# A streaming encoder layer on one core: order of the operand casts behind the last gate blocks, a tile ahead of the first branch products, the steps of operand loads, and a place for one copied sum

## The chip, the cores and the metric

The kernel runs on one core of one Trainium2 chip. The metric is the device time of one execution in microseconds; the time of a kernel is the median of its runs. Lower is better.

## The reference

One encoder layer for a prompt of 1024 tokens and a sample group of 32 tokens (1056 columns together), model width 1024, all in 32-bit floats. What matters here, cut down:

```python
h = rms_norm(x)
z = h @ w_in                        # q, k, v of branch A; q, f, i, og of branch B; gate_A, gate_B
ya = sliding_window_attention(...)  # branch A
yb = hgrn2_recurrence(...)          # branch B
mix = sigmoid(ga) * (ya @ w_br_a) + sigmoid(gb) * (yb @ w_br_b)
x = x + rms_norm(mix @ w_out)
a, u = split(rms_norm(x) @ w_up)    # each 2816 wide
x = x + rms_norm((gelu(conv3(a)) * u) @ w_down)
x = x + (p @ w_ple) * sigmoid(x @ w_ple_gate)
```

The change touches three borders: the end of the gate columns of `z`, the start of `ya @ w_br_a`, and the start of `rms_norm(x) @ w_up`.

## The kernel before, in words

**Products.** Every 32-bit operand is split in two parts, `hi` (a rounded cast, made by ACT) and `lo` (the rest, made by DVE), and a product of two such operands is three matmuls: hi by hi, hi by lo, lo by hi. Large products are taken as 2 x 2 blocks in a scheme of seven block products and some sums of operands and results, instead of eight. The columns (tokens) stand in four groups of H = 264. One product of a weight block with one group is 4 k-slices x 3 = 12 matmuls of 128 x 264.

**Gates.** `stream` (L252) multiplies a block of gate columns in two halves of 12 matmuls 128 x 384, into one PSUM bank; these appear in the trace as L205, L206, L207 with the banks called X, Y, Z. Behind a block, `gate_out` has ACT evict the bank with a tanh (L297, tile `gt`) and SP store it (L298, to `tb_d`). After each half m, `stream` runs the functions that `small[m]` lists. The last three blocks are `stream(tail[3:], small)`, so m counts 0 to 5, and what `small` lists is the preparation of branch A, put between the gates' own work:

- `a_prepare(n)` (L1514): makes weight blocks up to the n-th ready; a block is a cast on ACT (L1522, `wt<-wa`) and a subtraction on DVE (L1523). The raw blocks `wa` lie two to a tile in two tiles, which SP loads (L1512) when DVE has done with the blocks that lay there; `wt` has eight tiles. The order of the blocks is `A_ORDER` (L1496): for each column block c the products i = 0, 1, 2, later for each c the products 3 to 6.
- `a_split(i, p)` (L1540): operand i of column half p is split in place, a cast on ACT (L1537, `oa<-oa`) and a subtraction on DVE (L1538).
- `a_load(i, p)` (L1531): the load of an operand, L1534. The first five are issued by POOL before the stream, the rest by SP.

ACT, DVE and SP each run their instructions in the order in which they are listed for them; whoever waits holds what is listed behind it. `both` (L1543) lets the listed work of ACT and DVE be placed right behind what these engines were given last.

**Branch A.** `a_unit(ph, c, tps)` (L1593) takes two PSUM tiles X and Y of two banks each from the pool `pa` (tag `st`, three buffers). In phase 0 it makes product i = 0 in X, i = 1 in Y, and then adds i = 2 to X (L1620 hi·hi, L1622 hi·lo, L1624 lo·hi). Between the first and the third, ACT copies X to `as` (L1629), so that the product i = 2 cannot start before this copy; DVE makes `R` from Y and `as` (L1631), and after i = 2 it forms `ta` (L1634), a gate read back by SP (L1590, a ring of four tiles) times the product, which POOL stores to `mx_d` (L1635). The fifth load of `ta` needs the tile of the first, so it waits for the landing of the first store to `mx_d`. The units of phase 0 run in the order (c=0, p=0), (c=1, p=0), (c=0, p=1), (c=1, p=1), then c=2 and c=3 with both halves. In what follows X0 and Y0 are the tiles of the first unit, X1 and Y1 those of the second, and so on, and X1·i2 is the third product of the second unit. On PE the 12 matmuls of a product may be laid in pieces between those of others: before the change the order is X0·i0 12, Y0·i1 12, X1·i0 8, X0·i2 12, X1·i0 4, Y1·i1 12, X1·i2 12, so that 32 matmuls stand ahead of the first that needs `as`. After each product, `beside` runs the functions listed by `during(step, ...)` (L1676 ff): loads and splits of the operands 3 to 6.

**Up.** The up product has units of the same kind (L2304 hi·hi, L2305 hi·lo, L2306 lo·hi), with three PSUM tiles X, Y, Z. In `after` (L2311) ACT copies the first product from X to `s1c` (L2315), DVE makes `U2` (L2317), `nU3` (L2322) and from it a part of `us` (L2324). `s1c`, `U2`, `nU3` and `t12` are the four quarters of one page called `Sp` (L2178), which at this point holds an operand that DVE reads for the last time in L1902, the subtraction behind the cast of L1901. Just before, ACT copies a bank of the product with `w_ple` (L1948) and just behind it comes the output of the previous residual, `x` (ACT L1883, DVE L1888).

Of the kernel before, what the change touches and what calls it, by code (L numbers as in the profile page):

```python
# [10 lines left out]
F32 = mybir.dt.float32  # L11
# [3 lines left out]
ALU = mybir.AluOpType  # L15
AX = mybir.AxisListType

P = 128
# [12 lines left out]
H = 264  # L31
# [28 lines left out]
def layer_kernel(  # L60
# [21 lines left out]
    def right(name, bufs=1):  # L82
        return tc.tile_pool(name=name, bufs=bufs, side="right", reuse_waits="tile")

    dma, gdma = nc.sync.dma_start, nc.gpsimd.dma_start
    V, S, G, E = nc.vector, nc.scalar, nc.gpsimd, nc.tensor

    def behind(*engines):

        st = ExitStack()  # L90
        for e in engines:
            ins = next(i for i in reversed(nc.cur_bb.bb.instructions) if i.engine == e.engine)
            st.enter_context(tc.issue_after(ins))
        return st
# [185 lines left out]
    def unit(out):  # L280

        cell = []

        def get_w():
            if not cell:
                cell.append(next_w())
            return cell[0]
        return [(get_w, g, out) for g in range(3)]
# [4 lines left out]
    def gate_out(dst):  # L293
        def out(g, b):
            o, n = GR[g]
            t = gtile()
            S.activation(t[:, :n], b[:, :n], AF.Tanh, scale=0.5)  # L297
            dma(dst[:, o:o + n], t[:, :n])  # L298
        return out
# [17 lines left out]
    with right("ap") as ap:  # L317
# [279 lines left out]
        def pinned(f, *engines):  # L597
            with behind(*engines):
                f()
# [333 lines left out]
        blocks, small = [(lambda w=w: w, 2, out) for w, out in zip(ws, outs)], {}  # L933
# [125 lines left out]
    def b_prepare(n):  # L1059

        while n_b[0] < min(n + 1, 8 * NB):
            u, i = divmod(n_b[0], 8)
            if i == 0:
                if u not in raw_b:
                    b_raw(u)
                gens_b[u] = b_parts(u)
            next(gens_b[u])
            if i == 4 and u + 1 < NB:
                b_raw(u + 1)
            n_b[0] += 1  # L1070

    small = {2 * n: [lambda n=n: pinned(lambda: b_prepare(n), V)] for n in range(3)}
# [14 lines left out]
    with right("bp") as bp:  # L1087
# [309 lines left out]
        pieces, small = [], {}  # L1397
# [72 lines left out]
        u, v = (unit(gate_out(dst)) for dst, _ in GATES[14:])  # L1470
# [9 lines left out]
    def page(pool, n, shape, name):  # L1480

        s = f"{'r' if pool is rp else 'l'}{n}"
        s = home.get(s, s)
        return (rp if s[0] == "r" else lq).tile(shape, F32R, tag=f"pg{s[1:]}", name=nm(name))

    def page_at(s, shape, name):
        return page(rp if s[0] == "r" else lq, s[1:], shape, name)
# [40 lines left out]
    def a_page(i, p):  # L1528
        opa[i, p] = page_at(at_a[i][p], [P, 2, 4, H], "oa")

    def a_load(i, p, queue=dma):  # L1531
        t = opa[i, p]
        src = sa_d[i][:, :, p] if i in sa_d else ya_v[:, min(i, 1), i // 6][:, :, p]
        queue(t[:, 1].bitcast(F32), src)  # L1534
# [8 lines left out]
    def both(f, *a):  # L1543
        with behind(S, V):
            f(*a)

    small = {}
    first_a = [(i, p) for p in range(2) for i in range(3)]
    for i, p in [(3, 0), (3, 1), *first_a[::-1]]:
        a_page(i, p)  # L1550
    for i, p in first_a[:5]:
        a_load(i, p, gdma)
    for m, (i, p) in enumerate(first_a[:5]):
        small[m + 1] = [lambda i=i, p=p: both(a_split, i, p)]
    for n, m in enumerate((0, 0, 2, 3, 4, 5)):
        small.setdefault(m, []).append(lambda n=n: both(a_prepare, n))
    small[3].append(lambda: a_load(2, 1))
    stream(tail[3:], small)
    lctx.close()
# [4 lines left out]
    with right("mp") as mp:  # L1564
# [5 lines left out]
        pa = qctx.enter_context(  # L1570
            tc.tile_pool(name="pa", bufs=1, space=PSUM, reuse_waits="tile"))
# [2 lines left out]
            return bank(pt, "tr", 2)  # L1574

        Ra, Rb, Ya, Yb = [None] * 4, [None] * 4, [None] * 4, [None] * 4
        R_ = page_at("l6", [P, 4, 2, H], "R").bitcast(F32)

        tps_a = [(0, (0,)), (1, (0,)), (0, (1,)), (1, (1,)), (2, (0, 1)), (3, (0, 1))]
# [18 lines left out]
        def a_unit(ph, c, tps=(0, 1), ws=None, beside=None):  # L1598
# [9 lines left out]
            for n, i in enumerate(OPS[ph]):  # L1608
# [8 lines left out]
                for p in tps:  # L1617
                    o, x = t[:, p, 0:H], opa[i, p]
                    for k in range(4):
# [5 lines left out]
                                 skip_group_check=True)  # L1625
                x, r = t[:, sl, 0:H], R_[:, c, sl]
                if i == 0:
# [28 lines left out]
        def during(s, f, *a):  # L1656
            steps_a.setdefault(s, []).append((f, a))
# [12 lines left out]
            limit[0] = n_mix  # L1670
            both(load_next)

        for n, (i, p) in enumerate((i, p) for i in (4, 5, 6) for p in range(2)):
            a_page(i, p)
            during(2 * n, a_load, i, p)
            during(9 + n + n // 2, both, a_split, i, p)  # L1676
        for p in range(2):
            during(p, a_load, 3, p)
        for n, (i, p) in enumerate(((2, 1), (3, 0), (3, 1))):
            during(2 * n + 1, both, a_split, i, p)  # L1680
        for n in range(4):
            during(18 + n, y_load, n // 2, n % 2)
            during(23 + n, both, y_split, n // 2, n % 2)
# [104 lines left out]
    fo = foctx.enter_context(right("fo"))  # L1788
# [385 lines left out]
    octx.close()  # L2174
    fctx = ExitStack()
    fp = fctx.enter_context(right("fp"))
    us0 = fp.tile([P, T + 2], F32, tag="a", name="us0", bufs=2)[:, 0:T]
    Sp = page(lq, 3, [P, 4, 2, H], "Sp")  # L2178
    s1c, U2, nU3, t12 = (Sp[:, i].bitcast(F32) for i in range(4))
# [107 lines left out]
    def up_unit(u):  # L2287
# [4 lines left out]
        us4 = us.rearrange("p (a h c) -> p a h c", a=2, h=2)  # L2292
# [15 lines left out]
        def v(t, ps):  # L2308
            return t[:, ps[0]:ps[-1] + 1, 0:H]

        def after(i, ps):  # L2311
            x, y, zz = v(X, ps), v(Y, ps), v(Z, ps)
            sl = slice(ps[0], ps[-1] + 1)
            if i == 0:
                S.copy(s1c[:, sl], x)  # L2315
            elif i == 1:
                V.tensor_tensor(U2[:, sl], s1c[:, sl], y, op=ALU.subtract)  # L2317
            elif i == 2:
                V.tensor_tensor(ab[:, 2:2 + T].rearrange("p (a h c) -> p a h c", a=2, h=2)[:, sl, 0, :],
                                x, rb4[:, sl, 0, :], op=ALU.mult)  # L2320
            elif i == 3:
                V.tensor_tensor(nU3[:, sl], y, s1c[:, sl], op=ALU.subtract)  # L2322
            elif i == 4:
                V.tensor_tensor(us4[:, sl, 1, :], nU3[:, sl], zz, op=ALU.subtract)  # L2324
            elif i == 5:
                V.tensor_tensor(us4[:, sl, 0, :], y, s1c[:, sl], op=ALU.subtract)
            elif i == 7:

                S.copy(t12[:, sl], zz)
            elif i == 8:  # L2330
                V.tensor_tensor(nU3[:, sl], nU3[:, sl], t12[:, sl], op=ALU.add)
            else:
                V.tensor_tensor(t12[:, sl], U2[:, sl], zz, op=ALU.add)
# [465 lines left out]
    y = ys[1, 3]  # L2799
# [55 lines left out]
def build(shapes):  # L2855
    import concourse.bacc as _bacc

    nc = _bacc.Bacc("TRN2", target_bir_lowering=False, num_devices=1)
    args = [nc.dram_tensor(f"in_{n}_dram", s, F32, kind="ExternalInput").ap() for n, s in shapes]
    for i, shape in enumerate(_OUTS):  # L2860
        args.append(nc.dram_tensor(f"out_{i}_dram", shape, F32, kind="ExternalOutput").ap())
    with tile.TileContext(nc) as tc:
        layer_kernel(tc, *args)
    return nc
# [10 lines left out]
```

## Time and profile before

| | |
|---|---|
| median of 3 runs | 1948.23 us (1948.08, 1948.23, 1950.14) |
| the profiled execution's own time | 1950.0 us |
| its span | 1948.2 us (1.8 us lie outside the span) |
| PE busy | 1927.2 us, 99% |
| DVE, ACT, POOL busy | 75%, 52%, 16% |
| granted TensorE clock | 0.999 |

Times in the trace count from the start of the span. A row of the timeline has start, duration, engine, line, operation, output and inputs, and in brackets how long the engine was idle before it and what released it. A row of SP or POOL with `DMA_DIRECT2D` is the issue of a transfer, not the transfer.

### The profile page before, as it was taken

What the parts mean: (1) busy time and instruction counts of PE and PEld (TensorE: products, weight loads), DVE (VectorE), ACT (ScalarE), POOL (GpSimd) and SP (SyncE); (2) the same over time, 40 slices, a digit from 0 to 9 for tenths busy, and PEclk for the clock granted to TensorE, in tenths of its full rate; (3) what the DMA queues carried; (4) which work ended last, traced back from release to release, by engine and by line L of the source; (5) the groups of instructions that cost most, each with busy time, mean ns of one, the idle gap of its engine ahead of it and who ended that gap; (6) DMA issues with size and microseconds to landing.
All of it is one profiled execution on the core that took longest, in us unless ns stands there. A gap on an engine that the chain in (4) does not pass through costs nothing. (4 is left out here: it accounts for less than half of the span.)

```text
span 1948.2 us, 38057 instructions
## 1 busy us (share of the span) xinstructions
PE 1927.2 (99%) x14619; PEld 1910.0 (98%) x14619; DVE 1453.3 (75%) x3160; ACT 1012.4 (52%) x2182; POOL 307.3 (16%) x419
## 2 busy tenths in 40 slices
PE   8999999999999999999999999999999999999998
PEld 8999999999999999999999999999999999999998
DVE  6777777788888888657755778788787786768872
ACT  7667777666666666553324763333333336534432
POOL 2111111010101110100001123343543410000000
PEclk9999999999999999999999999999999999999999
DMA  8534543434637563487748582444565357654342
GB/s 269 156 108 122 139 121 97 139 104 103 155 113 166 96 120 75 124 292 226 219 148 289 182 290 92 140 131 152 131 147 148 104 179 235 220 185 153 115 132 87
DMA packets 310507, 302.19 MB, mean 155 GB/s; under 512 B 14293, under 2 KB 276344, under 8 KB 310325
## 3 DMA queue, kind: packets, MB, share of 16 engines
q1 hardware_dynamic: 277269, 229.57, 37.8%
q0 software_dynamic: 32928, 70.14, 15.8%
q8 instruction: 115, 1.88, 0.4%
q14 instruction: 67, 0.55, 0.1%
q10 hardware_dynamic: 128, 0.06, 0.0%
HBM read 213.48 MB, written 115.16 MB: 169 GB/s over the span
## 5 line engine op out<-in xcount | busy, mean ns | idle before, releaser
L2304 PE MATMUL st<-op,wt 128*128 128x264 f32 x1232 | 348.8, 283 | 2.1 <-ACT Sp L2315 1.4
L2306 PE MATMUL st<-op,wt 128*128 128x264 f32 x1232 | 349.7, 284 | 0.0
L2305 PE MATMUL st<-op,wt 128*128 128x264 f32 x1232 | 347.7, 282 | 0.0
L2304 PEld LDWEIGHTS st<-op,wt 128*128 128x128 f32 x1232 | 231.2, 188 | 3.5 <-ACT Sp L2315 2.0
L2305 PEld LDWEIGHTS st<-op,wt 128*128 128x128 f32 x1232 | 231.3, 188 | 0.0
L2306 PEld LDWEIGHTS st<-op,wt 128*128 128x128 f32 x1232 | 230.8, 187 | 0.0
L2428 PE MATMUL st<-dop,wt 128*128 128x264 f32 x616 | 174.4, 283 | 1.4 <-ACT S L2443 1.4
L2430 PE MATMUL st<-dop,wt 128*128 128x264 f32 x616 | 174.3, 283 | 0.0
L2429 PE MATMUL st<-dop,wt 128*128 128x264 f32 x616 | 173.9, 282 | 0.0
L1972 ACT CAST wt<-wu 128x512 fp32r<-128x512 f32 x126 | 76.0, 619 | 177.7 <-POOL wu L1981 70.9
L205 PE MATMUL mm<-La,wh 128*128 128x384 f32 (+1 forms) x480 | 158.2, 330 | 0.0
L206 PE MATMUL mm<-Lb,wh 128*128 128x384 f32 (+1 forms) x480 | 155.3, 324 | 0.6 <-DVE Lb L781 0.4
L207 PE MATMUL mm<-La,wl 128*128 128x384 f32 (+1 forms) x480 | 154.9, 323 | 0.1
L1973 DVE TENSOR_TENSOR wt<-wu,wt 128x512 fp32r<-128x512 f32 x126 | 86.4, 694 | 44.9 <-ACT wt L1972 44.9
L2428 PEld LDWEIGHTS st<-dop,wt 128*128 128x128 f32 x616 | 115.6, 188 | 1.9 <-ACT S L2443 1.6
L2429 PEld LDWEIGHTS st<-dop,wt 128*128 128x128 f32 x616 | 115.7, 188 | 0.0
L2430 PEld LDWEIGHTS st<-dop,wt 128*128 128x128 f32 x616 | 115.4, 188 | 0.0
L2078 ACT CAST wt<-wd 128x512 fp32r<-128x512 f32 (+1 forms) x84 | 49.1, 586 | 91.7 <-PE st L2430 71.9
L206 PEld LDWEIGHTS mm<-Lb,wh 128*128 128x128 f32 x480 | 90.4, 189 | 1.7 <-DVE Lb L781 1.4
L207 PEld LDWEIGHTS mm<-La,wl 128*128 128x128 f32 x480 | 90.2, 188 | 0.5 <-DVE wl L756 0.5
L1119 PE MATMUL G<-La,wt 128*128 128x288 f32 x288 | 90.4, 314 | 0.0
L205 PEld LDWEIGHTS mm<-La,wh 128*128 128x128 f32 x480 | 90.2, 188 | 0.2
(602 smaller groups left out, 6240.8 us busy)
## 6 DMA issues: line engine op xcount, KB each, us to landing
wu<-in_w_up_dram SPq DMA_DIRECT2D x42, 512.0 KB
wu<-in_w_in_dram SPq DMA_DIRECT2D x36, 512.0 KB
w_d<-in_w_down_dram POOLq DMA_DIRECT2D x24, 704.0 KB, 6.9
a_d<-Up SPq DMA_DIRECT2D x22, 528.0 KB
wr<-in_w_in_dram SPq DMA_DIRECT2D x21, 512.0 KB
s_d<-sm SPq DMA_DIRECT2D x40, 264.0 KB
dop<-s_d SPq DMA_DIRECT2D x16, 528.0 KB
wr<-in_w_out_dram SPq DMA_DIRECT2D x16, 512.0 KB
```

Source lines behind the costliest of these rows:

```text
L205: E.matmul(ps, wh, a, start=first and n == 0, stop=False)
L206: E.matmul(ps, wh, b, start=False, stop=False)
L207: E.matmul(ps, wl, a, start=False, stop=last and n == len(ks) - 1)
L1119: E.matmul(o, wh, x[0][k], start=first and k == 0, stop=False, skip_group_check=True)
L1972: S.copy(t[:, 0], src)
L1973: V.tensor_tensor(t[:, 1], src, t[:, 0].bitcast(F32), op=ALU.subtract)
L2304: E.matmul(o, wh, xh, start=first and k == 0, stop=False, skip_group_check=True)
L2305: E.matmul(o, wh, xl, start=False, stop=False, skip_group_check=True)
L2306: E.matmul(o, wl, xh, start=False, stop=k == 3, skip_group_check=True)
L2428: E.matmul(o, wh, xh_, start=first and k == 0, stop=False, skip_group_check=True)
L2429: E.matmul(o, wh, xl_, start=False, stop=False, skip_group_check=True)
L2430: E.matmul(o, wl, xh_, start=False, stop=k == ng - 1, skip_group_check=True)
```

## The change

Four edits. (1) `small` is filled by one table instead of two rules. (2) A tile `st_gate` is taken from the pool `pa` ahead of the first unit, and is not used. (3) The loads of the operands 3 to 6 and their splits get other steps; the loads of operand 3 move from steps 0 and 1 to 1 and 3, the others from 0, 2, 4, 6, 8, 10 to 4, 5, 6, 8, 9, 11. (4) For the first half of the first up unit, the copied sum `s1` lies in a tile of its own (`s10`, in a buffer of the pool `fo` that was used for squares) instead of a quarter of `Sp`.

```diff
-    for m, (i, p) in enumerate(first_a[:5]):
-        small[m + 1] = [lambda i=i, p=p: both(a_split, i, p)]
-    for n, m in enumerate((0, 0, 2, 3, 4, 5)):
-        small.setdefault(m, []).append(lambda n=n: both(a_prepare, n))
+    for m, at_m in enumerate(((0, 1, (0, 0), (1, 0)), ((2, 0), 2), ((0, 1),), ((1, 1), 3), (4,), (5,))):
+        small[m] = [lambda x=x: both(a_prepare, x) if isinstance(x, int) else both(a_split, *x)
+                    for x in at_m]
     small[3].append(lambda: a_load(2, 1))
...
+        pa.tile([P, 2, 512], F32, tag="st", name="st_gate", bufs=3)
...
-        for n, (i, p) in enumerate((i, p) for i in (4, 5, 6) for p in range(2)):
-            a_page(i, p)
-            during(2 * n, a_load, i, p)
-            during(9 + n + n // 2, both, a_split, i, p)
-        for p in range(2):
-            during(p, a_load, 3, p)
-        for n, (i, p) in enumerate(((2, 1), (3, 0), (3, 1))):
-            during(2 * n + 1, both, a_split, i, p)
+        for i in (4, 5, 6):
+            for p in range(2):
+                a_page(i, p)
+        for n, (i, p) in enumerate((i, p) for i in (3, 4, 5, 6) for p in range(2)):
+            during((1, 3, 4, 5, 6, 8, 9, 11)[n], a_load, i, p)
+            during((5, 7, 9, 10, 12, 13, 15, 16)[n], both, a_split, i, p)
+        during(1, both, a_split, 2, 1)
...
+    s10 = fo.tile([P, H], F32, tag="sqz0", name="s10")
...
+            s1 = s10[:, :].unsqueeze(1) if u == 0 and ps == (0,) else s1c[:, sl]
             if i == 0:
-                S.copy(s1c[:, sl], x)
+                S.copy(s1, x)
             elif i == 1:
-                V.tensor_tensor(U2[:, sl], s1c[:, sl], y, op=ALU.subtract)
+                V.tensor_tensor(U2[:, sl], s1, y, op=ALU.subtract)
```

The other two readers of `s1c` in `after` get `s1` in the same way.

What this makes of the programs: every engine has the same number of instructions before and after. PE, ACT, DVE and SP have other orders at the start of branch A, POOL the same order; from the middle of branch A on the programs differ in the place of `s1` alone. The first tile X0 lies in the same PSUM banks (2 and 3) in both programs, and its first matmul waits for the same semaphores of ACT.

On ACT, from the third weight block to the second `as`, the order before is this. `wt_10920`, `wt_10940`, `wt_10962`, `wt_10982`, `wt_11038` and `wt_11057` are blocks 3 to 8 in the order of `A_ORDER`; `oa_10852`, `oa_10851`, `oa_10850` and `oa_10849` are the operands (2, 0), (0, 1), (1, 1) and (2, 1); `gt` is the eviction of the last gate block, and the brackets name the semaphores that an instruction waits for (DMAHW and DMASW are transfers).

```order
L1522 CAST wt_10920<-wa_10876 128x512
L1537 CAST oa_10852<-oa_10852 128x1056 [waits DMASW6_49]
L1522 CAST wt_10940<-wa_10876 128x512 [waits DMAHW6_49]
L1537 CAST oa_10851<-oa_10851 128x1056 [waits DMASW7_49]
L1522 CAST wt_10962<-wa_10917 128x512 [waits DMAHW7_49]
L297 ACTIVATE gt_10977<-Z_10944 128x384 [waits DMAHW2_49,PE_49,Activation_49]
L1537 CAST oa_10850<-oa_10850 128x1056 [waits DMASW0_49]
L1522 CAST wt_10982<-wa_10917 128x512 [waits DMAHW0_49]
L1522 CAST wt_11038<-wa_10959 128x512 [waits DMAHW6_49]
L1537 CAST oa_10849<-oa_10849 128x1056 [waits DMAHW1_49]
L1629 COPY as_11031<-st_11017 128x264 [waits PE_49]
L1522 CAST wt_11057<-wa_10959 128x512 [waits DMAHW7_49]
```

And after, where `wt_10909`, `wt_10944`, `wt_10964`, `wt_10982`, `wt_11037` and `wt_11056` are blocks 3 to 8:

```order
L1522 CAST wt_10909<-wa_10876 128x512
L1537 CAST oa_10851<-oa_10851 128x1056 [waits DMASW7_49]
L297 ACTIVATE gt_10979<-Z_10948 128x384 [waits DMAHW2_49,PE_49,Activation_49]
L1537 CAST oa_10850<-oa_10850 128x1056 [waits DMASW0_49]
L1522 CAST wt_10944<-wa_10876 128x512 [waits DMAHW6_49]
L1522 CAST wt_10964<-wa_10906 128x512 [waits DMAHW7_49]
L1522 CAST wt_10982<-wa_10906 128x512 [waits DMAHW0_49]
L1629 COPY as_11032<-st_11018 128x264 [waits PE_49]
L1522 CAST wt_11037<-wa_10961 128x512 [waits DMAHW1_49]
L1537 CAST oa_10849<-oa_10849 128x1056
L1522 CAST wt_11056<-wa_10961 128x512 [waits DMAHW2_49]
L1629 COPY as_11095<-st_11075 128x264 [waits PE_49]
```

The eviction `gt` has moved ahead of two weight blocks, (2, 0) is done before this piece, and the first `as` stands ahead of block 7 (the first block of a raw tile that SP loads late) and of operand (2, 1).

On SP, from the raw tile of blocks 7 and 8 (`wa_10959`) to that of blocks 11 and 12 (`wa_11079`), the order before is this; `wa_11035` is the tile of blocks 9 and 10, `oa_11011` and `oa_11012` are operand 4.

```order
L1512 DMA wa_10959<-in_w_br_a_dram 128x4x128 [waits DVE_49]
L1512 DMA wa_10959<-wa_d_104 128x4x128 [waits DMAHW7_49]
L298 DMA tb_d_102<-gt_10977 128x384 [waits DMAHW0_49,Activation_49]
L1512 DMA wa_11035<-in_w_br_a_dram 128x4x128 [waits DMAHW1_49,DVE_49]
L1590 DMA ta_11005<-ta_d_87 128x264 [waits DMAHW2_49,PE_49]
L1590 DMA ta_11007<-ta_d_88 128x264 [waits DMAHW3_49]
L1590 DMA ta_11009<-ta_d_87 128x264 [waits DMAHW4_49]
L1534 DMA oa_11011<-sa_d_110 128x4x264 [waits DMAHW5_49]
L1512 DMA wa_11035<-in_w_br_a_dram 128x4x128 [waits DMAHW6_49]
L1590 DMA ta_11074<-ta_d_88 128x264 [waits DMAHW7_49]
L1534 DMA oa_11012<-sa_d_110 128x4x264 [waits DMAHW0_49,PE_49]
L1512 DMA wa_11079<-wa_d_104 128x4x128 [waits DMAHW1_49,DVE_49]
```

And after, with `wa_10961`, `wa_11034` and `wa_11077` as the tiles of blocks 7 and 8, 9 and 10, 11 and 12, and `oa_11012` as operand (4, 0):

```order
L298 DMA tb_d_102<-gt_10979 128x384 [waits Activation_49]
L1590 DMA ta_11006<-ta_d_87 128x264 [waits DMAHW7_49,PE_49]
L1590 DMA ta_11008<-ta_d_88 128x264 [waits DMAHW0_49]
L1512 DMA wa_10961<-in_w_br_a_dram 128x4x128 [waits DMAHW1_49,DVE_49]
L1512 DMA wa_10961<-wa_d_104 128x4x128 [waits DMAHW2_49]
L1590 DMA ta_11010<-ta_d_87 128x264 [waits DMAHW3_49]
L1512 DMA wa_11034<-in_w_br_a_dram 128x4x128 [waits DMAHW4_49,DVE_49]
L1512 DMA wa_11034<-in_w_br_a_dram 128x4x128 [waits DMAHW5_49]
L1590 DMA ta_11073<-ta_d_88 128x264 [waits DMAHW6_49]
L1534 DMA oa_11012<-sa_d_110 128x4x264 [waits DMAHW7_49]
L1590 DMA ta_11135<-ta_d_89 128x2x264 [waits DMAHW0_49,DMASW1_49,DVE_49]
L1512 DMA wa_11077<-wa_d_104 128x4x128 [waits DMAHW2_49,DMAHW1_49,DVE_49]
```

The load of blocks 7 and 8 has moved behind two `ta` loads, and the fifth `ta` load (`ta_11135`, which waits for a store of POOL, DMASW1) now stands ahead of the load of blocks 11 and 12; before, it stood behind it.

On PE the order after is X0·i0 12, Y0·i1 12, X1·i0 2, X0·i2 12, X1·i0 10, Y1·i1 12, X2·i0 8, X1·i2 12: 26 matmuls stand ahead of the first that needs `as`, and 68 ahead of the one that needs the second `as`.

At the start of the up product, ACT before has this order; `ple` is the last copy of the product with `w_ple`, `Sp_14698` the page with the quarter `s1c`, `x_14269` the residual's output.

```order
L1901 CAST op_14626<-z_13153 128x1056 [waits DVE_49]
L1901 CAST op_14629<-z_13153 128x1056
L1948 COPY ple_14663<-st_14678 128x528 [waits PE_49]
L2315 COPY Sp_14698<-st_14699 128x264 [waits DVE_49,PE_49]
L1883 ACTIVATE x_14269<-x_14269 128x1056 [waits DMASW4_49]
```

And after, with lines that stand one lower or higher in the file:

```order
L1900 CAST op_14627<-z_13154 128x1056 [waits DVE_49]
L1900 CAST op_14630<-z_13154 128x1056
L1947 COPY ple_14664<-st_14679 128x528 [waits PE_49]
L2316 COPY s_14698<-st_14701 128x264 [waits PE_49]
L1882 ACTIVATE x_14270<-x_14270 128x1056 [waits DMASW4_49]
```

Nothing has moved here; the copy no longer waits for DVE. On PE the first unit's products were X·i0 12, Y·i1 12, Z·i4 2, X·i2 12, Y·i3 12, Z·i4 10, Y·i5 12, Z·i6 12, and are now X·i0 12, Y·i1 12, X·i2 12, Y·i3 12, Z·i4 12, Y·i5 12, Z·i6 12.

More of the change, by code (lines that the diff above doesn't have):

```diff
@@ L2321, in after @@
             elif i == 3:
-                V.tensor_tensor(nU3[:, sl], y, s1c[:, sl], op=ALU.subtract)
+                V.tensor_tensor(nU3[:, sl], y, s1, op=ALU.subtract)
             elif i == 4:
@@ L2325, in after @@
             elif i == 5:
-                V.tensor_tensor(us4[:, sl, 0, :], y, s1c[:, sl], op=ALU.subtract)
+                V.tensor_tensor(us4[:, sl, 0, :], y, s1, op=ALU.subtract)
             elif i == 7:
```

## The prediction

> **What bounds the kernel now.** I read the page first, for the busiest engine:
>
> ```profile
> PE 1927.2 (99%) x14619; PEld 1910.0 (98%) x14619; DVE 1453.3 (75%) x3160; ACT 1012.4 (52%) x2182; POOL 307.3 (16%) x419
> ```
>
> PE works for 1927.2 of the 1948.2 us of the span. The change removes no matmul, so it can only win from the 21.0 us in which PE is idle. Next, PE's waits by line, at the lines that the change touches:
>
> ```profile
> PE st L1620 <- ACT as L1629: 1.6, 2, 1.4
> PE st L2304 <- ACT Sp L2315: 1.4, 2, 0.9
> ...
> PE st L1620 <- ACT gt L297: 1.3, 1, 1.3
> ...
> PE st L2304 <- DVE us L2324: 0.3, 1, 0.3
> ```
>
> That is 1.6 + 1.4 + 1.3 + 0.3 = 4.6 us, 0.24% of the time. Third, PE's timeline at the border from the gates to branch A:
>
> ```profile
> 843.95 0.33 PE L207 MATMUL Y<-La,wl 128*128 128x384 f32 x1
> ...
> 848.11 0.34 PE L207 MATMUL Z<-La,wl 128*128 128x384 f32 x1
> 849.77 0.39 PE L1620 MATMUL st<-oa,wt 128*128 128x264 f32 x1 [1.32 <-ACT gt L297]
> 850.00 0.28 PE L1622 MATMUL st<-oa,wt 128*128 128x264 f32 x1
> ...
> 853.64 0.28 PE L1622 MATMUL st<-oa,wt 128*128 128x264 f32 x1
> 855.27 0.39 PE L1620 MATMUL st<-oa,wt 128*128 128x264 f32 x1 [1.35 <-ACT as L1629]
> ...
> 875.13 0.39 PE L1620 MATMUL st<-oa,wt 128*128 128x264 f32 x1 [0.20 <-ACT as L1629]
> ```
>
> Three waits: for the eviction of the last gate block, for the first `as`, and a small one. From 850.00 to 853.64 there are 30 steps (matmuls 2 to 32 of the order), so a matmul costs 0.121 us; the first one after a wait is followed 0.23 later (849.77 to 850.00), so each wait costs 0.11 beyond itself.
>
> Why was ACT late? Its timeline there:
>
> ```profile
> 844.37 0.49 ACT L297 ACTIVATE gt<-Y 128x384 f32<-128x384 f32 x1 [2.79 <-PE Y L207]
> 844.75 1.07 ACT L1537 CAST oa<-oa 128x1056 fp32r<-128x1056 f32 x1
> 845.72 0.62 ACT L1522 CAST wt<-wa 128x512 fp32r<-128x512 f32 x1
> ...
> 848.71 0.61 ACT L1522 CAST wt<-wa 128x512 fp32r<-128x512 f32 x1
> 849.23 0.49 ACT L297 ACTIVATE gt<-Z 128x384 f32<-128x384 f32 x1
> ...
> 853.35 0.62 ACT L1522 CAST wt<-wa 128x512 fp32r<-128x512 f32 x1 [2.15 <-DMA wa<-in_w_br_a_dram]
> 853.88 1.07 ACT L1537 CAST oa<-oa 128x1056 fp32r<-128x1056 f32 x1
> 854.85 0.37 ACT L1629 COPY as<-st 128x264 f32<-128x264 f32 x1
> ```
>
> From 844.75 on ACT is busy without a gap, and the eviction of Z stands behind casts: it starts at 849.23, though PE's last matmul of Z ended at 848.45. The copy `as` stands behind the cast of block 7, which waits 2.15 us for its load, and behind another cast. In both places ACT does first what PE needs later.
>
> **Part 1: the eviction earlier.** On ACT an operand cast takes 0.97 to the next start (844.75 to 845.72), a block 0.52 (848.71 to 849.23), an eviction 0.38 (844.37 to 844.75). After, ACT does (1,0) at 844.75, (2,0) at 845.72, block 3 at 846.69, (0,1) at 847.21, and is free at 848.18. The earlier eviction started 0.09 after the end of its last matmul (843.95 + 0.33 to 844.37); so Z's starts at 848.54 and ends at 849.03. PE started 0.05 after it before, so 849.08 instead of 849.77: **0.69 saved**. The operands of these casts were loaded by POOL, which then stood idle for long (the row of 858.09 below), so (2,0) is there 0.5 us sooner. DVE's half of (2,0) and of block 3 is worked out below and is done by 848.9, before PE needs it.
>
> **Part 2: `as` ahead of block 7.** Behind the eviction ACT does (1,1) at 848.92, blocks 4, 5 and 6 at 849.89, 850.41 and 850.93, and `as` at 851.45, done at 851.82. PE, from 849.08, has 26 matmuls before it needs `as`: 849.08 + 0.11 + 26 x 0.121 = 852.34. So no wait is left. Before, PE's matmul 33 would have come at 853.76 and came at 855.27: 1.51 plus 0.11, **1.62 saved**.
>
> **Part 3: the up copy.** The rows of PE, ACT and DVE at that border:
>
> ```profile
> 1155.65 0.28 PE L2305 MATMUL st<-op,wt 128*128 128x264 f32 x1
> 1156.88 0.39 PE L2304 MATMUL st<-op,wt 128*128 128x264 f32 x1 [0.95 <-ACT Sp L2315]
> ...
> 1163.06 0.39 PE L2304 MATMUL st<-op,wt 128*128 128x264 f32 x1 [0.34 <-DVE us L2324]
> ```
>
> ```profile
> 1154.76 0.60 ACT L1948 COPY ple<-st 128x528 f32<-128x528 f32 x1
> 1156.44 0.38 ACT L2315 COPY Sp<-st 128x264 f32<-128x264 f32 x1 [1.07 <-DVE op L1902]
> ```
>
> ```profile
> 1153.93 2.42 DVE L1902 TENSOR_TENSOR op<-z,op 128x1056 fp32r<-128x1056 f32 x2 [1.06 <-ACT op L1901]
> ...
> 1158.81 1.26 DVE L1888 TENSOR_TENSOR x<-x 128x1056 f32<-128x1056 f32 x1 [1.53 <-ACT x L1883]
> 1160.10 0.43 DVE L2322 TENSOR_TENSOR Sp<-st,Sp 128x264 f32<-128x264 f32 x1
> ...
> 1162.58 0.42 DVE L2324 TENSOR_TENSOR us<-Sp,st 128x264 f32<-128x264 f32 x1
> ```
>
> The copy waited 1.07 for DVE to finish reading the page that it writes. With its own tile it goes when ACT is free: the `ple` copy ends at 1155.36, and on ACT the next start lies 0.1 ahead of such an end (the cast of 844.75 ends at 845.82, the next starts at 845.72). So it starts at 1155.25, 1.19 earlier. X·i2 then starts at 1155.69. The end is set by `us`, though: Z·i6 waits for it, and it stands on DVE behind L1888, which waits for ACT's `x`, next behind the copy, and whose own wait is for a store issued long before (1141.13):
>
> ```profile
> 1141.13 1.50 POOL L1851 DMA_DIRECT2D x_d<-x  x2 [2.15 <-DVE x L1850]
> ```
>
> That chain moves by the same 1.19, so Z·i6 starts at 1161.87 instead of 1163.06: **1.19 saved**. PE gets there at 1155.69 + 0.11 + 48 x 0.121 = 1161.61, so a wait of 0.26 stays: the 0.34 does not go.
>
> Gains: 0.69 + 1.62 + 1.19 = 3.50 us.
>
> **What these moves cost.** Three new things; their rows, DVE, then SP, ACT and POOL:
>
> ```profile
> 845.86 1.26 DVE L1538 TENSOR_TENSOR oa<-oa 128x1056 fp32r<-128x1056 f32 x1 [2.99 <-ACT oa L1537]
> 847.03 0.68 DVE L1523 TENSOR_TENSOR wt<-wa,wt 128x512 fp32r<-128x512 f32 x1
> ...
> 848.80 0.68 DVE L1523 TENSOR_TENSOR wt<-wa,wt 128x512 fp32r<-128x512 f32 x1
> ...
> 857.37 0.42 DVE L1634 SCALAR_TENSOR_TENSOR ta<-ta,st 128x264 f32<-128x264 f32 x1
> ```
>
> ```profile
> 849.51 0.39 SPq L1512 DMA_DIRECT2D wa<-in_w_br_a_dram  x1
> ...
> 863.92 0.52 SPq L1590 DMA_DIRECT2D ta<-ta_d  x1
> ...
> 881.23 0.38 SPq L1512 DMA_DIRECT2D wa<-in_w_br_a_dram  x1
> ```
>
> ```profile
> 884.53 0.62 ACT L1522 CAST wt<-wa 128x512 fp32r<-128x512 f32 x1 [0.17 <-DMA wa<-in_w_br_a_dram]
> ```
>
> ```profile
> 858.09 0.56 POOL L1635 DMA_DIRECT2D mx_d<-ta  x1 [30.92 <-DVE ta L1634]
> ```
>
> ```profile
> SPq L1590 <- DMA mx_d<-ta: 7.8, 3, 3.9
> ```
>
> (n1) *Blocks 7 and 8 come later.* SP may load them when DVE has done with block 4. Before, that was 848.80 + 0.68 = 849.48, and SP issued at 849.51. After, DVE does (1,0) at 845.86, then (2,0), block 3, (0,1), (1,1), block 4 at 1.17 an operand (845.86 to 847.03) and 0.60 a block (847.03 to 848.80 less one operand): block 4 at 851.14, done at 851.82. The load takes 3.30 (881.23 to 884.53) to 3.84 (849.51 to 853.35) from issue to cast, so block 7 is cast at 855.15 to 855.7, and then (2,1), block 8 and the second `as` follow, 0.52 + 0.97 + 0.52 + 0.37 = 2.38 later: 857.55 to 858.1. PE needs it after 68 matmuls, at 849.19 + 68 x 0.121 = 857.42. A wait of 0.1 to 0.7, with restart up to 0.8; none if the load is a little quicker. I take 0.4, between, nearer to the 3.30.
> [...]
>
> (n2) *The fifth `ta` load ahead of blocks 11 and 12.* It waits for the first store to `mx_d`, and before it was issued 5.83 after that store's issue (858.09 to 863.92). The store comes 0.72 after `ta` begins (857.37 to 858.09), and that 2.10 after the third product's start (855.27 to 857.37). After: 852.34 + 2.10 + 0.72 = 855.16, so the fifth load goes at 860.99 at the latest; the other end is that the store lands as soon as the quickest of these loads, 3.30, at 858.46. The blocks' load goes behind its 0.52, and block 11 is cast 3.30 to 3.84 later: 862.3 to 865.4. An operand cast and the fourth `as` follow, 0.52 + 0.97 + 0.37 = 1.86: 864.2 to 867.2. PE needs this `as` after 132 matmuls, 849.19 + 132 x 0.121 + 0.4 = 865.56. So 0 to 1.7; I take 0.3, as most of the stretch lies before the need.
>
> (n3) *The small wait at 875.13* stands behind a cast of operand 5, whose load stands behind another `ta` load as before. It may go with its restart (0.2 + 0.11 gained) or grow; the nearest row for growth is the 2.15 that ACT waited for a load at 853.35, of which 1.35 reached PE, 1.15 more than now. The stores and loads ahead of it move with PE, so I take 0.
>
> The loads of operand 3 at later steps cost nothing: on SP they keep their place, and their splits come later. The tile `st_gate` costs nothing: it issues no instruction, and X0 keeps its banks.
>
> Sum: 3.50 - 0.4 - 0.3 = **2.8 us**. The profiled execution would go from 1950.0 to 1947.2; the median of the runs shown lies 1.8 below it, so the median goes from 1948.23 to **1945.4**.
>
> **Rivals.** *New waits eat the gain.* n1 at 0.8 and n2 at 1.7 leave 1.0 (1947.2); with n3 at its 1.15 as well, it is a loss of 0.15 (1948.4). For it: each move of ACT's order makes DVE free a raw tile later. Against: all of it hangs on loads that take the longer of the two times. Chance 0.20.
> *All waits go.* The loads come in time (0 for n1 and n2), and 875.13 (0.31) and 1163.06 (0.34 + 0.11 less what of it part 3 holds) go too: 3.50 + 0.31 + 0.39 = 4.2, 1944.0. For it: with PE earlier by 2 us the stores come earlier too. Against: the two new loads stand later on SP than before. Chance 0.15.
> *Slower: SP held by a store.* SP issues in order, and `ta` loads that wait for stores to `mx_d` (7.8 us in 3 waits, 3.9 the longest) now stand ahead of the loads of blocks 11 and 12 and of operands 5 and 6. If two such waits of 3.9 reach PE whole, 2 x 3.9 - 3.50 = +4.3, 1952.5. It decides once a store's landing is later than the blocks that PE still has: PE has 132 matmuls, 16 us, before the first. In before PE met none of the 7.8. Chance 0.04.
> [...]
> *The other banks do part X0 from the gates*, against the built order: PE would go on at 848.28 instead of 849.08, 0.8 more, 1943.9. Chance 0.02, since the first matmul waits on ACT as before.
>
> **How the numbers follow.** Forecast 0.59, new waits 0.20, all waits gone 0.15, slower 0.04, banks 0.02. The range 1944.0 to 1948.4 runs from "all gone" to the far end of "new waits"; forecast and new waits alone hold 0.79, so the lower end has to reach to the third. About 0.2% (3.9 us) is what a measurement of this kernel can tell from no change: runs of before lie 2.06 us apart. The forecast and the new waits stay within it (0.79); all gone and banks pass it (4.2 and 4.3): faster 0.17; slower 0.04.
>
> **What would show it.** In the profile after: no wait of L1620 for the first `as`; L297's wait shorter by 0.7; the first matmul of branch A 0.6 to 1.0 behind the last of Z; the up unit's wait for L2316 at most 0.2, and the one for `us` still there. A wait for the second and fourth `as` of a few tenths shows n1 and n2; none shows the third case. The forecast is wrong if PE waits over 1 us anywhere between 850 and 885, if PE's first wait is gone wholly (banks), or if ACT's `x` at the up border waits for its load, which would hold `us`.

## The result and the profile after

| | changed | before |
|---|---|---|
| median of 22 runs | 1953.23 us | 1950.01 us |
| lowest, highest | 1949.76, 1955.63 | 1948.06, 1954.85 |
| ratio, 95% interval | 1.0014 (1.0008 to 1.0021) | |
| profiled execution, span | 1950.3, 1948.6 us | 1950.0, 1948.2 us |

The change makes the kernel 0.14% slower, about 2.7 us (1.6 to 4.1), where a gain of 2.8 was forecast; the two medians themselves lie 3.2 apart. With 22 runs instead of 3, the median of before is 1950.01 and no longer 1948.23.

PE's waits in the profile after, at the same lines, and one at the very start of the program, which was 0.4 in before:

```profile
PE st L1620 <- ACT as L1629: 2.3, 2, 1.4
...
PE mm L654 <- DMA x<-in_x_prompt_dram: 1.2, 1, 1.2
...
PE st L1620 <- ACT gt L297: 0.6, 1, 0.6
...
PE st L2304 <- ACT s L2316: 0.4, 1, 0.4
...
PE st L2304 <- DVE Sp L2318: 0.2, 1, 0.2
```

The gate wait has fallen from 1.3 to 0.6, the copy's at the up border from 0.95 to 0.4; but the waits for `as` are 2.3 instead of 1.6, and they lie elsewhere. PE's timeline:

```profile
848.63 0.34 PE L207 MATMUL Z<-La,wl 128*128 128x384 f32 x1
849.60 0.39 PE L1620 MATMUL st<-oa,wt 128*128 128x264 f32 x1 [0.63 <-ACT gt L297]
...
857.85 0.28 PE L1622 MATMUL st<-oa,wt 128*128 128x264 f32 x1
858.17 0.39 PE L1620 MATMUL st<-oa,wt 128*128 128x264 f32 x1
...
867.11 0.39 PE L1620 MATMUL st<-oa,wt 128*128 128x264 f32 x1 [0.91 <-ACT as L1629]
...
876.09 0.39 PE L1620 MATMUL st<-oa,wt 128*128 128x264 f32 x1 [1.44 <-ACT as L1629]
```

The first `as` is no longer waited for. The second costs a little (0.32 from 857.85 to 858.17 instead of 0.12), the fourth 0.91, and the fifth, the first of column block 2, has grown from 0.20 to 1.44. What ACT did ahead of each:

```profile
849.06 0.49 ACT L297 ACTIVATE gt<-Z 128x384 f32<-128x384 f32 x1 [0.24 <-PE Z L207]
...
851.97 0.38 ACT L1629 COPY as<-st 128x264 f32<-128x264 f32 x1
855.73 0.62 ACT L1522 CAST wt<-wa 128x512 fp32r<-128x512 f32 x1 [3.38 <-DMA wa<-in_w_br_a_dram]
...
865.18 0.62 ACT L1522 CAST wt<-wa 128x512 fp32r<-128x512 f32 x1 [2.37 <-DMA wa<-wa_d]
...
874.46 1.07 ACT L1537 CAST oa<-oa 128x1056 fp32r<-128x1056 f32 x1 [1.85 <-DMA oa<-sa_d]
875.44 0.59 ACT L1629 COPY as<-st 128x528 f32<-128x528 f32 x1
```

The eviction now starts 0.09 behind PE's last matmul of Z (848.63 + 0.34) and no longer stands behind casts; `as` goes ahead of block 7, at 851.97. But the copy at 875.44, for which PE waits, stands behind the cast of operand (5,1), and that one waits 1.85 for its load, though PE doesn't need (5,1) until much later. SP in after, where the fifth `ta` load goes at 860.49, the sixth at 865.81 and the load of (5,1) at 867.37:

```profile
860.49 0.52 SPq L1590 DMA_DIRECT2D ta<-ta_d  x1
861.12 0.55 SPq L1512 DMA_DIRECT2D wa<-wa_d  x1
...
865.81 1.51 SPq L1590 DMA_DIRECT2D ta<-ta_d  x1
867.37 0.72 SPq L1534 DMA_DIRECT2D oa<-sa_d  x1
```

And its waits from 830 to 880:

```profile
SPq L1590 <- DMA mx_d<-ta: 8.5, 3, 4.2
```

In before, SP issued the load of (5,1) at 866.28, ahead of the sixth `ta` load:

```profile
866.28 0.63 SPq L1534 DMA_DIRECT2D oa<-sa_d  x1
867.01 0.65 SPq L1590 DMA_DIRECT2D ta<-ta_d  x1
```

There ACT's cast of it waited 1.14 and started at 873.51:

```profile
873.51 1.08 ACT L1537 CAST oa<-oa 128x1056 fp32r<-128x1056 f32 x1 [1.14 <-DMA oa<-sa_d]
```

PE's last matmul of Z ended at 848.45 in before and at 848.97 in after. Counted from there, the load of (5,1) is issued 0.57 later after the change and its cast starts 0.43 later, while PE gets to the matmul that needs `as` 0.80 earlier (876.09 - 1.44 against 875.13 - 0.20). The last two make up the 1.24 by which the wait has grown. At the up border, PE and ACT after:

```profile
1156.68 0.39 PE L2304 MATMUL st<-op,wt 128*128 128x264 f32 x1 [0.40 <-ACT s L2316]
...
1173.33 0.39 PE L2304 MATMUL st<-op,wt 128*128 128x264 f32 x1 [0.19 <-DVE Sp L2318]
```

```profile
1155.74 0.60 ACT L1947 COPY ple<-st 128x528 f32<-128x528 f32 x1
1156.23 0.39 ACT L2316 COPY s<-st 128x264 f32<-128x264 f32 x1
```

The copy goes 0.49 behind `ple`, as worked out, and the wait for `us` is gone as well; 17 us behind the copy's wait there is a new one for `U2` (L2318).

### The profile page after: what moved, and what is told of

It is laid out like the page before. It is cut to its first block, busy times and chain, and to the rows that moved or that the text cites. A ratio compares the mean times of both kernels' runs of the same rounds, so it can differ in the third digit from the quotient of the medians.

```text
span 1948.6 us, 38055 instructions
## 1 busy us (share of the span) xinstructions
PE 1927.8 (99%) x14619; PEld 1910.3 (98%) x14619; DVE 1453.7 (75%) x3160; ACT 1011.8 (52%) x2182; POOL 307.1 (16%) x419
```

## The experiments

Theory A: the place of the waiting `ta` loads on SP, ahead of loads on which ACT's casts and so an `as` hang, takes back what the casts gain. Rivals: B, the later casts free the raw weight tiles late; C, the loss lies at the up border; D, it came with the chip of the first timing; E, the loads are slow in themselves, since the DMA engines are full; F (beside A), a long wait lowers the granted clock. Parts 1 to 4 are here the four edits of the change. Each ratio is to runs of before on the same chip, with its 95% interval; "own" is the time of the profiled execution.

**e1_casts** (part 1 alone)

```diff
+    for m, at_m in enumerate(((0, 1, (0, 0), (1, 0)), ((2, 0), 2), ((0, 1),), ((1, 1), 3), (4,), (5,))):
```

> Only the order of the casts is changed (part 1), the loads keep their old steps and the copied sum its old place. Theory A (the loss comes from the place of the waiting ta loads on SP, which the load steps set): here the fifth ta load stands behind the weight blocks 11 to 14, so PE has no wait for the fourth as, the gate wait is about 0.6 and the first as wait is gone: 1.5 to 2.3 us below before. Rival B (the later casts free the raw weight tiles later, so blocks come late): 1 to 3 us above before, with waits for the second and fourth as near 859 and 867 as in after.

0.9999 (0.9991 to 1.0008), own 1949.96. The gate wait is 0.63 and the first `as` is not waited for, so both gains are there; new waits of 0.71 at 862.00 and 0.54 at 874.56 take back 1.25, less the 0.20 of before. No loss as B has it, and less gain than A.

**e2_loads** (part 3 alone)

```diff
+            during((1, 3, 4, 5, 6, 8, 9, 11)[n], a_load, i, p)
+            during((5, 7, 9, 10, 12, 13, 15, 16)[n], both, a_split, i, p)
```

> Only the load steps are changed (part 3). Theory A: the fifth ta load stands ahead of operand (4,1) and the sixth ahead of blocks 13 and 14, PE keeps its waits of 1.3 and 1.35 and gets new ones of 1 to 2 us between 860 and 880: 2 to 4 us above before. Rival B: no change within 0.5 us.

1.0003 (0.9994 to 1.0012), own 1952.46. The first `as` wait is 0.61 instead of 1.35, the one at 875.93 is 0.99 instead of 0.20. The load steps alone lengthen the later wait by 0.79, as A says, but the first wait falls by 0.74, and the time is level with before, where A expected 2 to 4 us above and B no change. This profile is longer than that of before for two other reasons: PE is 1.3 us later by 60 us, where the programs are the same, and in a stage that the change doesn't touch it goes at half clock (0.50 from 1619.22 to 1622.63), behind this wait (in before 1.42 there, and a clock of 1.00 from 1619 to 1624):

```profile
1618.57 0.39 PE L2427 MATMUL st<-dop,wt 128*128 128x264 f32 x1 [1.84 <-ACT S L2442]
```

**e3_sums** (part 4 alone)

```diff
-                S.copy(s1c[:, sl], x)
+                S.copy(s1, x)
```

> Only the copied sum has a tile of its own (part 4). Theories A and B: the wait of 0.95 for the copy falls to 0.2 or 0.4, something later gives a part back, 0.4 to 1.2 us below before. Rival C (the loss of a usual execution lies at the up border, not in branch A): 1 to 3 us above before.

0.9997 (0.9988 to 1.0006), own 1952.73. The wait for the copy is gone and 0.42 comes at `U2`. C finds no support. This profile is 2.7 us longer than that of before for another reason: by 60 us, where both programs are the same, PE is already 3.6 us later (rows of PE in the two traces set side by side); one of the waits there is for x_prompt, 1.1 against 0.4.

**e4_casts_sums** (parts 1 and 4)

```diff
+    for m, at_m in enumerate(((0, 1, (0, 0), (1, 0)), ((2, 0), 2), ((0, 1),), ((1, 1), 3), (4,), (5,))):
...
+    s10 = fo.tile([P, H], F32, tag="sqz0", name="s10")
```

> Parts 1 and 4 together, the old load steps. Theory A: the two gains add, 2 to 3.3 us below before, and this is the best of the four. Rival B: 0 to 2 us above before. Rival C: above casts alone by 1 to 3 us.

0.9997 (0.9988 to 1.0006), own 1948.08, with one wait of 0.59 at 861.34 left in branch A. Below before in the median (1949.45 to 1950.34), but not beyond its interval.

**e5_after_again** (the changed kernel, no edit)

> The changed kernel once more, timed on this chip beside before. Theory A (the waiting ta loads on SP, with both the casts and the load steps changed): its profile again has 2 to 3.5 us of waits for the fourth as and the first as of column block 2 between 858 and 878, and it is 1 to 4 us above before. Rival D (the loss came with the chip of the first timing, whose granted clock was 0.998 in 7 of 22 runs): within 1 us of before here, with clocks of 0.999 and 1.0.

1.0011 (1.0002 to 1.0020): it is slower on another chip too, so D falls. Waits of 0.90 and 1.74.

**e6_ta_on_pool** (after, with the `ta` loads issued by POOL)

```diff
-                dma(t[:, z_], ta_d[c_].rearrange("p (t h c) -> p h t c", t=2, h=2)[:, h_, z_])
+                gdma(t[:, z_], ta_d[c_].rearrange("p (t h c) -> p h t c", t=2, h=2)[:, h_, z_])
```

> After, but the ta loads of branch A are issued by POOL, so that SP holds no wait for a store to mx_d. Theory A: blocks 11 to 14 and operand 5 are issued 2 to 5 us sooner, the waits of 0.91 and 1.44 go or fall below 0.3, 1.5 to 3 us below after. Rival D or a loss that lies in the landing times of the loads themselves: the waits stay, within 0.5 us of after.

1.0002 (0.9993 to 1.0011), own 1950.57. PE's waits in branch A:

```profile
850.88 0.39 PE L1620 MATMUL st<-oa,wt 128*128 128x264 f32 x1 [1.40 <-ACT gt L297]
...
868.30 0.39 PE L1620 MATMUL st<-oa,wt 128*128 128x264 f32 x1 [1.15 <-ACT as L1629]
```

The wait near 876 is gone, as A has it; the one for block 11 stays (1.15, at 868.30), and the gate wait is back (1.40), since there the eviction waits for an earlier store of `gt`. So A holds for the larger wait, and not for the one at 867. The time came down to that of before (e5, on the same chip, has 1.0011).

**e7_casts_loads** (parts 1 and 3)

```diff
+    for m, at_m in enumerate(((0, 1, (0, 0), (1, 0)), ((2, 0), 2), ((0, 1),), ((1, 1), 3), (4,), (5,))):
...
+            during((1, 3, 4, 5, 6, 8, 9, 11)[n], a_load, i, p)
```

> Parts 1 and 3 without the copied sum's own tile. Theory A: branch A as in after (waits of 2 to 3.5 us between 858 and 878), 0.3 to 0.6 us above after, 2 to 4 above before. Rival C (the up border costs something in a usual execution): 1 to 3 us below after.

1.0014 (1.0005 to 1.0023), own 1953.4. The loss is there without part 4 and without the tile of part 2, and not with either of parts 1 and 3 alone: the casts bring PE forward, the load steps put operand 5 back. The wait at 877.00 is 2.34, and the mean granted clock of the profiled execution is 0.998 (0.999 in before).

**e8_after_look, e13_after_look, e14_after_look** (the changed kernel, three more profiles, no edit)

> The changed kernel, a further profile. Theory A: the sum of PE's waits in branch A varies from profile to profile by 1 us or more, since each hangs on when a store lands. Rival D: it repeats within 0.3 us, and what varies is the start of the program, where PE waits for x_prompt.

> The changed kernel, another profile. If theory A with theory F explains the loss: a wait of 1.4 to 2.4 us near 876, and where it is over 2 us, a pitch of 0.22 behind it; the time is 1950 to 1951 without and 1952 to 1956 with the lower clock.

> As for the run before it: the time and the clock behind the wait go together; a profile above 1952 us without a lower clock near 876 speaks against theory F as the missing part.

Own 1952.13, 1951.40 and 1951.43. PE in e8, from the wait to the end of the slow stretch:

```profile
875.29 0.39 PE L1620 MATMUL st<-oa,wt 128*128 128x264 f32 x1 [2.33 <-ACT as L1629]
...
876.50 0.35 PE L1620 MATMUL st<-oa,wt 128*128 128x264 f32 x1
876.65 0.42 PE L1622 MATMUL st<-oa,wt 128*128 128x264 f32 x1
876.87 0.42 PE L1624 MATMUL st<-oa,wt 128*128 128x264 f32 x1
...
879.95 0.30 PE L1622 MATMUL st<-oa,wt 128*128 128x264 f32 x1
```

The same stretch in the windows of e8 and of after; the third number from the end is the granted clock:

```profile
875.00:880.00 5.00, 4.71 (x26) 4.71 (x27) 3.67 (x5) 2.38 (x5) 0.00 (x0) 0.66 1.08 312
```

```profile
875.00:880.00 5.00, 3.91 (x32) 3.92 (x33) 2.96 (x3) 2.53 (x4) 0.00 (x0) 1.00 1.11 327
```

From 876.65 to 879.95 there are 15 steps of 0.22 us instead of 0.121: 1.5 us lost while PE counts as busy, which no table of waits shows. In e13 and e14 the waits are as long, but the clock is 1.00 from 875.42 to 878.83 in e13, and the mean of e14's whole span is 1.000:

```profile
876.52 0.39 PE L1620 MATMUL st<-oa,wt 128*128 128x264 f32 x1 [2.64 <-ACT as L1629]
```

```profile
877.03 0.39 PE L1620 MATMUL st<-oa,wt 128*128 128x264 f32 x1 [2.08 <-ACT as L1629]
```

So the wait varies from 1.44 to 2.64 in five profiles of one kernel (1.74 in e5), and F holds for some of the long waits, not for all; the last section sets the rows side by side.

**e9_op5_early** (after, the load of (5,1) two steps sooner; on SP it only changes places with the sixth `ta` load)

```diff
-            during((1, 3, 4, 5, 6, 8, 9, 11)[n], a_load, i, p)
+            during((1, 3, 4, 5, 6, 6, 9, 11)[n], a_load, i, p)
```

> After, with the load of operand (5,1) two steps sooner: on SP it stands ahead of the sixth ta load and no longer behind it, all else in the same order. Theory A (the cast of (5,1) waits for a load that SP holds behind a waiting ta load, and the as of column block 2 stands behind that cast): PE's wait near 876 falls from 1.4 to 2.3 us to below 0.8, the granted clock stays 1.00 there, 1.5 to 3.5 us below after. Rival E (the loads themselves are slow, since the DMA engines are full from 845 to 880): the wait stays within 0.5 us of after's.

0.9998 (0.9990 to 1.0007), own 1951.83. SP and PE:

```profile
868.10 1.25 SPq L1534 DMA_DIRECT2D oa<-sa_d  x1
869.45 1.45 SPq L1590 DMA_DIRECT2D ta<-ta_d  x1
```

```profile
877.45 0.39 PE L1620 MATMUL st<-oa,wt 128*128 128x264 f32 x1 [0.52 <-ACT as L1629]
```

The place of one load takes the wait from at least 1.44 to 0.52 and the time from 0.14% or 0.11% above before to level with it; A had expected 1.5 to 3.5 us less than after, which is what came. This is the strongest single test of A.

**e10_split_late** (after, (5,1) split two steps later, so that the copy `as` stands ahead of its cast)

```diff
-            during((5, 7, 9, 10, 12, 13, 15, 16)[n], both, a_split, i, p)
+            during((5, 7, 9, 10, 12, 15, 15, 16)[n], both, a_split, i, p)
```

> After, with the loads as they are, but operand (5,1) split two steps later, so that ACT does the as of column block 2 ahead of the cast that waits for (5,1). Theories A and E alike: the wait near 876 is gone (below 0.3), no lower clock, 2 to 4 us below after; the wait of 0.6 to 0.9 near 867 stays, since it hangs on block 11. If the wait stays, it was not this cast that held as.

1.0018 (1.0010 to 1.0027), own 1955.24: a miss. The wait near 876 is gone, so it was that cast which held `as`; but 20 us later PE and ACT show:

```profile
898.15 0.56 PE L1620 MATMUL st<-oa,wt 128*128 128x264 f32 x1 [3.51 <-DVE ac L1641]
```

```profile
896.05 0.62 ACT L1522 CAST wt<-wa 128x512 fp32r<-128x512 f32 x1 [8.88 <-DMA wa<-wa_d]
```

A weight block comes late, DVE's half of it holds `ac`, and PE waits 3.51, again with a lower clock behind it (0.80 from 895 to 900, 0.86 from 900 to 905). The later split moved other loads on SP (four loads of `Yb` now go ahead of that block's instead of two); which of them decides was not taken apart.

**e11_op5_late** (after, the load of (5,1) behind a load of operand 6)

```diff
+            during((1, 3, 4, 5, 6, 10, 9, 11)[n], a_load, i, p)
```

> After, with the load of (5,1) two steps later, behind a load of operand 6. Theory F (a wait of over about 2 us makes the granted clock fall to half for some 3.4 us, and that is the part of the loss that the profile of after does not show): the wait near 876 is 2.5 us or longer, the matmuls after it have a pitch of 0.22 instead of 0.12 for 3 to 4 us, which costs 1.4 to 1.8 us more. Without theory F: the pitch stays 0.12.

Own 1951.55. Not what was meant: in this program ACT's cast of (5,1) has moved behind the `as` as well, so there is no wait near 876, and one of 0.48 at 885.23. It says nothing on F, whose 2 us and 3.4 us are the author's estimates: the 2 us lie between the wait of 1.74 in e5, whose mean clock is 1.000, and that of 2.33 in e8, and the 3.4 us are e8's stretch at 0.50 (876.56 to 879.97). No run shows 2 us as a limit: behind 2.64 in e13 the clock is 1.00.

**e12_best** (parts 1 and 4, (5,1) split later)

```diff
+            during((9, 10, 12, 15, 15, 16)[n], both, a_split, i, p)
```

> Parts 1 and 4 with the old load steps, and (5,1) split later. Theory A: the gains of the casts (2.3) and of the sum's own tile (0.5) stay, less a wait of about 0.6 near 861: 1.5 to 2.8 us below before, the fastest of all.

1.0017 (1.0008 to 1.0026), own 1954.78: a miss too, with waits of 0.94 at 863.99 and of 1.35 at 897.57, near that of e10. In this profile they only use up the gains of branch A: PE's rows are 2.0 us behind those of before at the last matmul of Z and again at 900. PE's rows lose another 1.4 behind a wait of 1.97 at 1619.54, where the change touches nothing. Why a usual run is 3.3 us slower than before is not shown.

**e15_casts_sums2** (e4 again)

```diff
+    s10 = fo.tile([P, H], F32, tag="sqz0", name="s10")
```

> Parts 1 and 4 with the old load steps, timed once more. Theory A: 0.5 to 2.5 us below before, with PE waits of 0.6 at the gate and below 1 for one or two as, no lower clock. If it is level with before, the casts' gain is used up by waits for loads in usual executions too.

0.9997 (0.9988 to 1.0006), own 1949.69, waits of 0.70 at 862.52 and 0.45 at 895.46.

**e16_casts_sums_op5** (parts 1 and 4, both loads of operand 5 ahead of the fifth and sixth `ta` loads)

```diff
-            during(2 * n, a_load, i, p)
+            during((0, 2, 4, 4, 8, 10)[n], a_load, i, p)
```

> Parts 1 and 4, and both loads of operand 5 ahead of the fifth and sixth ta loads. Theory A: the wait near 875 is below 0.3, 1 to 3 us below before and at or below the run before it. Rival E (full DMA engines): no different from the run before it.

0.9993 (0.9984 to 1.0002), own 1949.12: nothing left near 875, and a wait of 0.95 at 863.26, for block 9, whose load stands behind one of operand 4.

**e17_queue and e18_queue_again** (as e16, and operand 4 loaded behind blocks 9 and 10)

```diff
-            during(2 * n, a_load, i, p)
+            during((2, 3, 4, 4, 8, 10)[n], a_load, i, p)
```

> Parts 1 and 4, loads of operand 4 two and one steps later than in before (behind blocks 9 and 10), both loads of operand 5 ahead of the fifth and sixth ta loads. Theory A: no PE wait for an as above 0.5 us between 850 and 885, gate wait 0.6, 2 to 3 us below before. Rival E (full DMA engines): a wait of 0.6 to 1 us moves to another as or block, 0.5 to 1.5 us below before.

> The same kernel once more, for a second profile and a narrower interval: theory A 2 to 3 us below before, rival E 0.5 to 1.5 us.

0.9988 (0.9979 to 0.9997) and 0.9988 (0.9980 to 0.9997), medians 1948.89 and 1948.44 to 1951.33: 2.3 us faster than before. PE's waits in branch A in e17:

```profile
849.34 0.39 PE L1619 MATMUL st<-oa,wt 128*128 128x264 f32 x1 [0.63 <-ACT gt L297]
...
866.02 0.39 PE L1619 MATMUL st<-oa,wt 128*128 128x264 f32 x1 [0.38 <-ACT as L1628]
```

And the windows from 865 to 880 in e17 and in after; the last two numbers are the busy share of the DMA engines and GB/s:

```profile
865.00:870.00 5.00, 4.62 (x39) 4.41 (x38) 4.71 (x6) 3.44 (x5) 0.00 (x0) 1.00 1.11 347
870.00:875.00 5.00, 5.00 (x43) 4.96 (x42) 2.75 (x5) 3.58 (x5) 0.54 (x1) 1.00 1.09 360
875.00:880.00 5.00, 5.00 (x43) 5.00 (x43) 3.90 (x6) 1.98 (x3) 0.00 (x0) 1.00 0.85 245
```

```profile
865.00:870.00 5.00, 4.09 (x34) 3.89 (x33) 4.00 (x6) 4.13 (x6) 0.54 (x1) 1.00 1.12 337
870.00:875.00 5.00, 4.65 (x39) 4.44 (x37) 3.32 (x5) 2.09 (x4) 0.54 (x1) 1.00 1.06 350
```

The DMA engines are as full from 865 to 875 in the one as in the other (1.11 and 1.09 against 1.12 and 1.06), and PE is busy for 4.62 and 5.00 of 5 us in e17, 4.09 and 4.65 in after. So it isn't the amount of transfer alone (E) that makes PE wait, but which transfer goes first.

## Why the prediction was wrong, point by point

**The gains at the first border were right.** The gate wait fell from 1.32 to 0.63, which is the 0.69 forecast, and the first `as` wait is gone (1.62). The rival in which the banks had moved is out: PE still waits for the eviction.

**Part 3 of the prediction, the up copy (edit 4), was mis-sized: 1.19 forecast, 0.43 measured.** PE's rows, matmul by matmul against those of before, go from 0.64 later to 0.19 earlier across the copy and the wait for `us`: 0.83. The rest of the 1.19 went because ACT's `ple` copy itself came 0.34 later against PE (1155.74 against 1154.76, with PE 0.64 later). Then 0.40 is given back at 1173.33, where DVE makes `U2` for the second half at its own pace. The prediction didn't look that far.

**n1 and n2.** The second `as` cost 0.31 (0.20 and the restart), forecast 0.4. The fourth cost 1.02 (0.91 and the restart), forecast 0.3 in a stretch of 0 to 1.7: inside, but in its far half. The reason given for 0.3, that most of the stretch lies before the need, doesn't hold by its own numbers: of 864.2 to 867.2, 1.4 of 3.0 us lie before 865.56. Block 11 was cast 4.06 after the issue of its load (861.12 to 865.18), not 3.30 to 3.84. In e6, with no `ta` load on SP, this wait stayed, and in e17, with the fifth `ta` load behind these blocks, 0.38 is left. Block 7 took 3.30 (852.43 to 855.73), as the rows had it.

**n3 was the step that failed.** "The stores and loads ahead of it move with PE, so I take 0." The wait measured 1.44, 1.74, 2.33, 2.64 and 2.08 in five profiles of the changed kernel, 0.20 before. They didn't move with PE: counted from the end of Z, PE came 0.80 earlier and the cast of (5,1) 0.43 later. The order on SP did change there: the load of (5,1) stood ahead of the sixth `ta` load and now stands behind it, and the rows for that lay in the program, a few rows below those shown with the change. The rival "SP held by a store" named this queue, these operands and this kind of wait, and had a chance of 0.04. Its argument against, that in before PE met none of the 7.8 us, is weak: PE was 0.80 later there, and the 0.20 at 875.13 was the sign that operand 5 came just in time. The sign set in advance, a wait of over 1 us between 850 and 885, is what came. Bringing PE forward there turns each us into waiting, unless the loads come forward too.

**The clock was left out.** The wait of 2.33 in e8 is followed by a stretch at half the clock (0.50 from 876.56 to 879.97), 1.5 us more; behind the 3.51 in e10 the clock is 0.80 from 895 to 900 and 0.86 from 900 to 905; the profiled execution of e7, with a wait of 2.34, has a mean of 0.998. The mean granted clock was 0.998 or lower in 17 of the 55 timed runs of the kernels with parts 1 and 3 both changed and later waits of that kind (7 of 22 of the changed kernel, 2 of 11 in e5, 4 of 11 each in e7 and e10), in 1 of 11 each of e6 and e12, and in none of the 99 of e1, e2, e3, e4, e9, e15, e16, e17 and e18. A mean of 0.999 doesn't rule such a stretch out, as the profile of e2 shows (0.999 over the span, 0.50 from 1619.22 to 1622.63).

**What the sum makes.** PE's rows set against those of before, from the last matmul of Z to 900 us, show branch A as a whole slower in all five profiles of the changed kernel: by 0.4 in after, 0.6 in e5, 2.2 in e8, 1.1 in e13 and 0.8 in e14. From there to 1200 us, across the up border, 0.3 to 0.7 comes back. By the terms, with gains of 0.69, 1.62 and 0.43 and the 0.31 of n1, after has 1.02 + 1.24 in new waits and comes to 0.2 below before; e8, with 0.59 + 0.11, 2.33 - 0.20 and 1.5 by the clock, to 1.9 above. The timed runs are 2.1 to 2.7 above. Much of what is missing goes with the clock: of the 33 timed runs of the changed kernel, those of e5 included, the 7 with a mean clock of 1.000 have a median of 1951.0, the 17 with 0.999 one of 1952.3, and the 9 with 0.998 one of 1955.0; of the 129 runs of before beside the experiments, 60 have 1.000 (median 1950.3), 66 have 0.999 (1950.8) and 3 have 0.998. In which stage the runs without a trace lost their clock stays open. That the loss hangs on the same load is shown by e9, which takes all of it away and has no run at 0.998.

**Another slip.** The time of the rival with other banks, 1943.9, leaves out n1 and n2; with them it would be 1944.6.

## What to carry to other kernels

When a border is made faster, list for the next 30 us every load whose landing a cast waits for, with the rows of the issuing queue ahead of it; a wait of 0.2 us there is no small cost, it says that the stage behind is just supplied (0.20 at 875.13 in before, 1.44 at 876.09 in after). On a queue that issues in order, as SP's rows of after show it (`ta` at 860.49, `wa` at 861.12, `ta` at 865.81, `oa` at 867.37), put what is needed first ahead of anything that waits for a store, and on the engine that casts, count a cast whose operand may be late as a wait of all that stands behind it (1.85 at 874.46 in after, with `as` at 875.44 behind it). Read every row of the order that moved, not only those around the first gain: the change of two neighbours on SP was worth the whole result here.

## What the runs showed of the hardware

The clock first, as the rows show it. Behind the wait of 2.33 us in e8 PE's step is 0.22 us instead of 0.121 from 876.65 to 879.95, 1.2 us after PE had restarted; behind the wait of 1.84 in e2 the clock is half as well. The rows of e8 and of e2 (length, then PE busy; the third number from the end is the clock):

```profile
876.56:879.97 3.41, 3.41 (x18) 3.41 (x18) 3.33 (x5) 1.14 (x2) 0.00 (x0) 0.50 1.07 295
```

```profile
1619.22:1622.63 3.41, 3.41 (x18) 3.41 (x18) 2.78 (x7) 1.56 (x4) 0.00 (x0) 0.50 0.78 297
```

And that of e13, whose wait of 2.64 ends at 876.52:

```profile
875.42:878.83 3.41, 2.31 (x19) 2.31 (x20) 1.35 (x2) 2.03 (x3) 0.00 (x0) 1.00 0.87 264
```

So the length of the wait alone doesn't tell the clock: 1.84 is followed by 0.50 in e2, and 2.64 by 1.00 in e13. What decides is not shown.

The load of (5,1), 128x4x264 against the 128x4x128 of a weight block, took 7.1 us from issue to cast in after (867.37 to 874.46), with a busy share of the DMA engines of 1.12 from 865 to 870 and 1.06 from 870 to 875, and 7.2 in before (866.28 to 873.51), with shares of 0.81 and 1.07 there. The 3.30 to 3.84 of a weight block were taken from rows with a share of 0.60 (880 to 885) and 0.65 (850 to 855) in before.

The start of the program differs by up to 3.6 us from execution to execution with the same instructions (e3 against before at 60 us), so a single profile's span says nothing on a change of 2 us; the rows at the place do.
